# Half-rotary embedding on one core: all large transfers in one queue, six resident tiles, scratch in PSUM, tables loaded from GpSimd

## The chip, the cores and the metric

The kernel runs on one core of one Trainium2 chip. The metric is the device time of one execution in microseconds (us). The kernel before takes 162.42 us, the median of six runs (162.1 to 162.7).

A core has several engines that run side by side. Here only four matter: VectorE (DVE in the profile) does all the arithmetic; SyncE (its queue is SPq), ScalarE (ACTq) and GpSimd (POOL) issue transfers between the chip's main memory (DRAM) and the core's working memory (SBUF). Every transfer is cut into packets, which 16 DMA engines move. PSUM is a second, smaller memory of the core.

## The reference

`x` has 16 x 512 x 16 x 64 elements in float32 (33.55 MB); `cos` and `sin` have 512 x 32. Only the first 32 of the 64 elements of a head are rotated, and of each table only the first 16 columns are used. The other 32 elements are copied.

```python
batch, seq, heads, dim = x.shape          # 16, 512, 16, 64
half_dim = dim // 2                       # 32
x1, x2 = x[..., :half_dim], x[..., half_dim:]
cos = cos[None, :, None, :]; sin = sin[None, :, None, :]
rotated_first  = x1[..., :16] * cos[..., :16] - x1[..., 16:] * sin[..., :16]
rotated_second = x1[..., :16] * sin[..., :16] + x1[..., 16:] * cos[..., :16]
return np.concatenate([rotated_first, rotated_second, x2], axis=-1)
```

All of `x` must be read once and all of the output, which is as large, written once: 67.1 MB in all.

## The kernel before

**Tiling.** Each of the 128 partitions takes eight consecutive positions of the sequence (`K = 8`), that is 8 x 16 x 64 floats, 32 KB in one contiguous piece. A tile `x_t` is 128 such partitions, 4.19 MB (the profile's 4096 KB), and there are `T = 8` tiles. A tile goes in by one load (L58), is rotated in place, and goes out by one store (L73).

**Tables.** `cos` and `sin` are loaded into `stage`, 64 partitions x 1 KB each, by two transfers that ScalarE issues (L41, L42). Four copies on VectorE (L48) spread the 16 used columns over `table`, 128 partitions wide and with each set of columns twice in a row. `C` and `Sn` are views of it.

**Arithmetic.** Each tile is worked in two halves of `KC = 4` positions. For each half VectorE makes two products over 128 x 2048 elements, `a_t` = x1 x cos (L65) and `b_t` = x1 x sin (L66), and then a difference (L67) and a sum (L70) over 128 x 1024 elements, which write the rotated values back into `x_t`. `a_t` and `b_t` have one buffer each, in SBUF.

**Order and waits.** The program is written tile by tile, and every wait follows from the data. Loads are issued by SyncE, stores by ScalarE, so they lie in two queues: q1 holds the loads, q10 the stores and, ahead of them, the two table loads. Within one queue the order is that of issue. `x_t` has five buffers. So the first five loads need no buffer to come free, and load 5 (counting from 0) waits until store 0 has landed, load 6 for store 1, and load 7 for store 2.

**Names that the prediction uses.** Load t and store t are the transfers of tile t, L58 and L73 of the kernel before. "Landing" is the moment at which a transfer's completion is seen.

Of the kernel before, what the change touches and what calls it, by code (L numbers as in the profile page):

```python
# [1 line left out]

# [4 lines left out]


@with_exitstack
def kernel(  # L10
    ctx: ExitStack,
    tc: tile.TileContext,
    x: bass.AP,
    cos: bass.AP,
    sin: bass.AP,
    out: bass.AP,
):
    nc = tc.nc
    fp32 = mybir.dt.float32
    P = 128  # L20
    B, S, H, D = x.shape
    Q = D // 4
    HF = D // 2


    K = 8
    T = B * S // (P * K)
    PB = S // K
    REP = P // PB

    xf = x.rearrange("b s h d -> (b s h d)").rearrange("(t p f) -> t p f", t=T, p=P)
    of = out.rearrange("b s h d -> (b s h d)").rearrange("(t p f) -> t p f", t=T, p=P)
    cosf = cos.rearrange("(p k) j -> p (k j)", k=K)
    sinf = sin.rearrange("(p k) j -> p (k j)", k=K)

    const_pool = ctx.enter_context(tc.tile_pool(name="const", bufs=1))
    x_pool = ctx.enter_context(tc.tile_pool(name="xp", bufs=5))
    ab_pool = ctx.enter_context(tc.tile_pool(name="abp", bufs=1))

    stage = const_pool.tile([PB, 2, K, HF], fp32)  # L40
    nc.scalar.dma_start(out=stage[:, 0].rearrange("p k j -> p (k j)"), in_=cosf)  # L41
    nc.scalar.dma_start(out=stage[:, 1].rearrange("p k j -> p (k j)"), in_=sinf)  # L42


    table = const_pool.tile([P, 2, K, 2, Q], fp32)
    for r in range(REP):
        for t in range(2):
            nc.vector.tensor_copy(  # L48
                out=table[r * PB : (r + 1) * PB, t],
                in_=stage[:, t, :, 0:Q].unsqueeze(2).to_broadcast((PB, K, 2, Q)),  # L50
            )
    C = table[:, 0].rearrange("p k c j -> p k (c j)")
    Sn = table[:, 1].rearrange("p k c j -> p k (c j)")

    KC = 4
    for t in range(T):
        x_t = x_pool.tile([P, K, H, D], fp32)
        nc.sync.dma_start(out=x_t.rearrange("p k h d -> p (k h d)"), in_=xf[t])  # L58
        for k0 in range(0, K, KC):
            x1 = x_t[:, k0 : k0 + KC, :, 0:HF]  # L60
            c = C[:, k0 : k0 + KC].unsqueeze(2).to_broadcast((P, KC, H, HF))
            s = Sn[:, k0 : k0 + KC].unsqueeze(2).to_broadcast((P, KC, H, HF))
            a_t = ab_pool.tile([P, KC, H, HF], fp32)
            b_t = ab_pool.tile([P, KC, H, HF], fp32)
            nc.vector.tensor_mul(out=a_t[:], in0=x1, in1=c)  # L65
            nc.vector.tensor_mul(out=b_t[:], in0=x1, in1=s)  # L66
            nc.vector.tensor_sub(  # L67
                out=x1[:, :, :, 0:Q], in0=a_t[:, :, :, 0:Q], in1=b_t[:, :, :, Q:HF]
            )
            nc.vector.tensor_add(  # L70
                out=x1[:, :, :, Q:HF], in0=a_t[:, :, :, Q:HF], in1=b_t[:, :, :, 0:Q]
            )
        nc.scalar.dma_start(out=of[t], in_=x_t.rearrange("p k h d -> p (k h d)"))  # L73


# [1 line left out]
_INS = ['x', 'cos', 'sin']  # L77
_OUTS = [((16, 512, 16, 64), 'float32')]


# [23 lines left out]
```

## Time and profile before

| What | Value |
|---|---|
| Median of six runs | 162.42 us (162.1 to 162.7) |
| The profiled execution's own time | 162.44 us |
| Its span, from first to last instruction | 160.7 us, so that 1.7 us lie around it |
| VectorE busy | 110.8 us (69%), 68 instructions |
| One product over 128 x 2048 (L65, L66) | 2292 and 2285 ns |
| One difference or sum over 128 x 1024 (L67, L70) | 1226 and 1220 ns |
| Data moved | 33.69 MB read, 33.55 MB written, 419 GB/s over the span |
| Load of a tile, median from issue to landing | 33.9 us |
| Store of a tile, median from issue to landing | 31.3 us |
| Table loads, from issue to landing | 11.6 us (cos), 16.4 us (sin) |

The page of the profile cuts the span into 40 equal slices. In each slice a digit gives the busy share in tenths, for an engine or for the 16 DMA engines together, and the line GB/s gives what they moved. Bytes of a packet are counted where the packet starts, so that rates over very short stretches jump; over several microseconds they level out. The share of a queue is the time that its packets took, as a share of the time of 16 DMA engines.

### The profile page before, as it was taken

To read this page: it belongs to the slowest core of one execution; us is meant where nothing else is said; L and a number is where in the kernel's file an instruction comes from. 1 tells how busy PE (TensorE), PEld (TensorE's weight loads), DVE (VectorE), ACT (ScalarE), POOL (GpSimd) and SP (SyncE) were. 2 spreads that over 40 slices of the span, in tenths; PEclk is the share of its full clock that TensorE was granted. 3 is DMA by queue.
4 is the path that set the end of the run, shared out by engine and by line. 5 is a ranking of instruction groups with operands and counts; after the bars stand their busy time and mean duration, and the time that the engine had idled before them with its cause. 6 is when DMAs were issued, how large, how long until landed. Compare 5 with 4: busy or idle time off the path is not lost.

```text
span 160.7 us, 155 instructions
## 1 busy us (share of the span) xinstructions
DVE 110.8 (69%) x68; POOL 0.2 (0%) x4
## 2 busy tenths in 40 slices
DVE  0001599999999999999997799609994099940000
POOL 0000000000000000000000000000000000000000
DMA  7999999999999999999999999999999999999993
GB/s 237 424 400 408 392 465 441 400 465 441 400 449 457 400 416 473 416 392 498 416 392 481 432 392 465 449 392 465 434 400 465 441 400 457 449 400 449 441 416 139
DMA packets 2465, 67.25 MB, mean 419 GB/s; under 512 B 288, under 2 KB 416, under 8 KB 416
## 3 DMA queue, kind: packets, MB, share of 16 engines
q1 hardware_dynamic: 1152, 33.55, 49.2%
q10 hardware_dynamic: 1312, 33.69, 48.6%
q14 instruction: 1, 0.01, 0.0%
HBM read 33.69 MB, written 33.55 MB: 419 GB/s over the span
## 4 chain that ended last, share of the span: by engine, by line
DMA 53%; DVE 30%; issue 4%; DVEq 1%; ACTq 0%; SPq 0%
DMA x_t<-in_x_dram 21%; DMA out_dram<-x_t 21%; DVE b_t L66 11%; DMA stage<-in_sin_dram 10%; DVE a_t L65 10%; DVE x_t L70 5%; DVE x_t L67 4%; DVEq L99 1%; ACTq L41 0%; DVE table L48 0%; SPq L58 0%; DVEq L65 0%
## 5 line engine op out<-in xcount | busy, mean ns | idle before, releaser
L65 DVE TENSOR_TENSOR a_t<-x_t,table 128x2048 f32<-128x2048 f32 x16 | 36.7, 2292 | 13.8 <-DMA x_t<-in_x_dram 13.4
L66 DVE TENSOR_TENSOR b_t<-x_t,table 128x2048 f32<-128x2048 f32 x16 | 36.6, 2285 | 0.0
L67 DVE TENSOR_TENSOR x_t<-a_t,b_t 128x1024 f32<-128x1024 f32 x16 | 19.6, 1226 | 0.6
L70 DVE TENSOR_TENSOR x_t<-a_t,b_t 128x1024 f32<-128x1024 f32 x16 | 19.5, 1220 | 0.0
L48 DVE COPY table<-stage 64x256 f32<-64x256 f32 x4 | 1.1, 286 | 17.1 <-DMA stage<-in_cos_dram 12.4
L88 POOL MEMSET const-bfloat16-1.0<- 128x1 bf16 x1 | 0.1, 101 | 0.0
L88 POOL MEMSET const-uint8-127<- 128x1 uint8 x1 | 0.1, 101 | 0.0
L88 POOL MEMSET const-float32-0.0<- 128x1 f32 x1 | 0.1, 98 | 0.2 <-issue 0.2
L88 POOL MEMSET const-float32-1.0<- 128x1 f32 x1 | 0.1, 98 | 0.0
## 6 DMA issues: line engine op xcount, KB each, us to landing
x_t<-in_x_dram SPq DMA_DIRECT2D x8, 4096.0 KB, 33.9
out_dram<-x_t ACTq DMA_DIRECT2D x8, 4096.0 KB, 31.3
stage<-in_cos_dram ACTq DMA_DIRECT2D x1, 64.0 KB, 11.6
stage<-in_sin_dram ACTq DMA_DIRECT2D x1, 64.0 KB, 16.4
```

Of the source, the lines that this page charges most:

```text
L48: nc.vector.tensor_copy(out=table[r * PB : (r + 1) * PB, t], in_=stage[:, t, :, 0:Q].unsqueeze(2).to_broadcast((PB, K, 2, Q)),)
L65: nc.vector.tensor_mul(out=a_t[:], in0=x1, in1=c)
L66: nc.vector.tensor_mul(out=b_t[:], in0=x1, in1=s)
L67: nc.vector.tensor_sub(out=x1[:, :, :, 0:Q], in0=a_t[:, :, :, 0:Q], in1=b_t[:, :, :, Q:HF])
L70: nc.vector.tensor_add(out=x1[:, :, :, Q:HF], in0=a_t[:, :, :, Q:HF], in1=b_t[:, :, :, 0:Q])
L88: nc = _bacc.Bacc("TRN2", target_bir_lowering=False, num_devices=1)
L99: with _tile.TileContext(nc) as tc:
```

## The change

All tile transfers, loads and stores, are issued by SyncE into one queue. The first six loads are issued ahead of everything else. Then the order is store 0, store 1, load 6, store 2, load 7, store 3, and the remaining stores. Six buffers of `x_t` instead of five. Load 6 takes the buffer of tile 0 and so needs store 0, load 7 needs store 1.

`a_t` is gone: the product with sin comes first, into `b_t`, and the product with cos is then made in place in `x_t`. `b_t` lies in PSUM, with two buffers. The table loads are issued by GpSimd instead of ScalarE.

```diff
+    NB = 6
...
-    x_pool = ctx.enter_context(tc.tile_pool(name="xp", bufs=5))
-    ab_pool = ctx.enter_context(tc.tile_pool(name="abp", bufs=1))
+    x_pool = ctx.enter_context(tc.tile_pool(name="xp", bufs=NB))
+    b_pool = ctx.enter_context(tc.tile_pool(name="bp", bufs=2, space=bass.MemoryType.PSUM))
...
-    nc.scalar.dma_start(out=stage[:, 0].rearrange("p k j -> p (k j)"), in_=cosf)
-    nc.scalar.dma_start(out=stage[:, 1].rearrange("p k j -> p (k j)"), in_=sinf)
+    nc.gpsimd.dma_start(out=stage[:, 0].rearrange("p k j -> p (k j)"), in_=cosf)
+    nc.gpsimd.dma_start(out=stage[:, 1].rearrange("p k j -> p (k j)"), in_=sinf)
...
+    tiles = []
+
+    def load(t):
+        x_t = x_pool.tile([P, K, H, D], fp32, name="x_t")
+        nc.sync.dma_start(out=x_t.rearrange("p k h d -> p (k h d)"), in_=xf[t])
+        tiles.append(x_t)
+
+    for t in range(NB):
+        load(t)
     for t in range(T):
-        x_t = x_pool.tile([P, K, H, D], fp32)
-        nc.sync.dma_start(out=x_t.rearrange("p k h d -> p (k h d)"), in_=xf[t])
+        x_t = tiles[t]
         for k0 in range(0, K, KC):
...
-            a_t = ab_pool.tile([P, KC, H, HF], fp32)
-            b_t = ab_pool.tile([P, KC, H, HF], fp32)
-            nc.vector.tensor_mul(out=a_t[:], in0=x1, in1=c)
+            b_t = b_pool.tile([P, KC, H, HF], fp32)
             nc.vector.tensor_mul(out=b_t[:], in0=x1, in1=s)
+            nc.vector.tensor_mul(out=x1, in0=x1, in1=c)
             nc.vector.tensor_sub(
-                out=x1[:, :, :, 0:Q], in0=a_t[:, :, :, 0:Q], in1=b_t[:, :, :, Q:HF]
+                out=x1[:, :, :, 0:Q], in0=x1[:, :, :, 0:Q], in1=b_t[:, :, :, Q:HF]
             )
             nc.vector.tensor_add(
-                out=x1[:, :, :, Q:HF], in0=a_t[:, :, :, Q:HF], in1=b_t[:, :, :, 0:Q]
+                out=x1[:, :, :, Q:HF], in0=x1[:, :, :, Q:HF], in1=b_t[:, :, :, 0:Q]
             )
-        nc.scalar.dma_start(out=of[t], in_=x_t.rearrange("p k h d -> p (k h d)"))
+        nc.sync.dma_start(out=of[t], in_=x_t.rearrange("p k h d -> p (k h d)"))
+        if t >= 1 and t - 1 + NB < T:
+            load(t - 1 + NB)
```

## The prediction

> **What bounds the kernel now.** I read the busy shares in 40 slices first, then the queues, then windows of the transfers at the start, in the middle and at the end, and last the waits of VectorE.
>
> ```profile
> DVE  0001599999999999999997799609994099940000
> DMA  7999999999999999999999999999999999999993
> q1 hardware_dynamic: 1152, 33.55, 49.2%
> q10 hardware_dynamic: 1312, 33.69, 48.6%
> ```
>
> VectorE has holes and the DMA engines have none: only the first and the last slice are not full. The two queues' shares add up to 97.8% of 160.7 us, 157.2 us of packets. All that an order of transfers could win lies in the remaining 3.5 us and in packets that take longer than they must. The chain of waits names DMA (53%) and DVE (30%), but a share there doesn't make VectorE a bound: where the chain runs along VectorE (18 to 60 us), the DMA engines are full all the same.
>
> ```profile
> 0.00:1.60 1.60, 0.00 (x0) 0.20 (x4) 1.00 0.00 0
> 1.60:2.60 1.00, 0.00 (x0) 0.00 (x0) 1.00 1.92 524
> 2.60:3.50 0.90, 0.00 (x0) 0.00 (x0) 1.00 0.00 0
> ...
> 32.00:128.00 96.00, 82.38 (x49) 0.00 (x0) 1.00 1.00 432
> ...
> 158.50:160.70 2.20, 0.00 (x0) 0.00 (x0) 1.00 0.00 0
> ```
>
> In the windows the last two columns are DMA share and GB/s; a packet counts where it starts. Nothing starts for 1.6 us. Then 16 packets start (524 GB/s x 1 us = 16 x 32 KB), one for each engine, and the next only after 3.5 us. A packet usually takes 1.21 us (below), so the first takes about 0.7 us longer. In the middle 432 GB/s flow with loads and stores mixed: a tile of 4.19 MB, eight packets on each engine, takes 9.7 us. After 158.5 us nothing moves; those 2.2 us are the last store's completion and the program's end.
>
> What a packet costs, alone and mixed, is in the queues' view of four stretches (0 to 20, 20 to 35, 60 to 120, 142 to 158 us):
>
> ```profile
> q1 hardware_dynamic: 240, 7.34, 90.9%
> q10 hardware_dynamic: 160, 0.13, 2.0%
> ...
> q1 hardware_dynamic: 233, 6.59, 102.0%
> ...
> q10 hardware_dynamic: 448, 13.11, 50.6%
> q1 hardware_dynamic: 446, 13.04, 50.4%
> ...
> q10 hardware_dynamic: 224, 6.82, 98.6%
> ```
>
> Divide the bytes by 32,768 for the number of data packets; share x length x 16 engines is their time. Loads at the start: 0.909 x 20 x 16 / 224 = 1.299 us. Loads alone: 1.02 x 15 x 16 / 201 = 1.218. Mixed: stores 0.506 x 960 / 400 = 1.214, loads 0.504 x 960 / 398 = 1.216. Stores alone: 0.986 x 256 / 208 = 1.213. So a queue by itself runs at the speed of two, in either direction, within 0.4%.
>
> The sum for the kernel before: start 1.6, plus 128 packets on each engine x 1.214 = 155.4, plus the excess of the first 14 loads on each engine, 14 x 0.085 = 1.2, plus the tables' own packets, 2.0% of 20 us = 0.4, plus the end 2.2: 160.8, against the span of 160.7. Of the 1.2, about 0.7 is the first packet; the other 0.5 stands beside the tables' small packets.
>
> **What the Trainium skill says.** "DMA: Bandwidth & Descriptors", section "Issuing engines are not separate DMA queues": transfers from SyncE, ScalarE and GpSimd all run on the same 16 engines and interleave; several issuers save only issue time. The trace agrees (the prices above). Its section "Queues, rings and completion order": an engine goes round its queues packet by packet, and data descriptors carry no barrier. The trace agrees: 64 KB of cos land after 11.6 us, since each small packet waits for a packet of x. Its section "SWDGE vs HWDGE vs iDMA": GpSimd writes its descriptors in software, in packets of preferably up to 4096 bytes. No run here shows it yet. "VectorE: DVE Perf Modes", section "The perf-mode tier table": fp32 tensor_tensor with 2048 elements runs at one element per cycle, 2293 ns, from SBUF, and also at one with an operand in PSUM. The trace has 2292 ns for SBUF and nothing for PSUM.
>
> **The change part by part.** *One queue.* The bytes stay the same. I follow the order with 9.7 us a tile. Loads 0 to 5 fill the engines until 1.6 + 1.2 + 0.4 + 6 x 9.7 = 61 us. VectorE starts as before at 18.3 and needs 13.85 us a tile (2 x 6.93, from one L65 to the next but one half), so store 0 is issued at 32 and store 1 at 46, both before the loads run out: no hole. Store 0 moves from 61 to 71, store 1 to 81. Load 6 waits for store 0's landing: the last store lands at 142.4 + 17.4 = 159.8, some 1.5 us after its last packet, so load 6 is issued at about 73, 8 us ahead of store 1's end. What stands behind it on SyncE's queue is store 2, then load 7, and so on; none is due before 81. Store 2 was ready at 60 and is issued right after load 6. Load 6 moves until 90, store 2 until 100; load 7 waits for store 1's landing (82), is issued 18 us early, and moves until 110; stores 3, 4, 5, 6 end at 120, 129, 139, 149. Tile 4 is computed by 88, tile 5 by 101, tile 6 (load landed at 92) by 115, tile 7 (load landed at 112) by 129, against the 149 at which store 7 can begin. The engines have work throughout, with 20 us in hand at the end. Issue itself costs 0.34 us a transfer on SyncE and has those 8 us as cover. So the two long waits that go (loads for stores, 75.4 us in the queue's own waits; VectorE for loads, 13.4) were worth nothing: full DMA engines stood beside them, and what is late next is again the engines' work.
>
> Two small differences remain. Loads run alone for six tiles, 48 packets on each engine, instead of until 36 us, some 28: 20 x 0.004 = +0.1 us. And the direction turns inside one queue five times (load 5 to store 0, 1 to 6, 6 to 2, 2 to 7, 7 to 3). The trace has turns only between two queues, and there at every packet without cost. From below a turn costs nothing, since the mixed price is that of stores alone; from above, the pipeline empties as at the start, 0.7 us each, 3.5 in all. I take 0: descriptors have no barrier, and load follows load within 1.218 us a packet, completion included.
>
> *Tables from GpSimd.* Now they cost 0.4 of own packets and 0.5 of stretched neighbours. Fewer, larger packets would stretch fewer neighbours: from -0.9 (all inside the first packet's 0.7 us and the start) to +0.9 (software descriptors double it). I take -0.2, half of the stretching's share. If they land later, VectorE starts later: the cover is 20 us, so up to a start at 38 nothing happens. GpSimd's queue holds only its four memsets (0.2 us). What its set-up and close add outside the span I put at 0, at most 1 us.
>
> *Scratch in PSUM and the product in place.* Still four instructions a half with the same shapes. The difference waits for the product just before it, as now (gaps of 0.02 us). The sum may now wait for the difference and lose its 0.08 us of overlap: 16 x 0.08 = 1.3 us. Of the four, three touch PSUM; price 0, the upper end twice the duration (a gain would be hidden, so the lower end is 0 too). Under the 20 us of cover, three in each of 16 halves may each grow by 0.4 us before it counts. The sixth buffer costs nothing and only lets load 5 go early.
>
> Sum: +0.1 - 0.2 = -0.1 on the profiled 162.44, which stands at the median of 162.42: 162.3 us.
>
> **Rivals.** *A, the forecast: the transfers bound both, all packets at their old price.* 161.9 to 162.9 with the unknown of the tables and of GpSimd's close; chance 0.62, of it 0.17 faster, 0.30 the same, 0.15 slower. *B, slower: turns in one queue.* At each of the five turns a DMA engine drains before it reads the other way. At half the upper price, 0.35 us, +1.75: 164.1; at the full one 165.9. It decides from 0.09 us a turn. For it: the first packet's 0.7 us shows that filling the pipeline costs; against it: mixed packets have no excess. 0.20 with what a wait of SyncE may add in the same place. *C, faster: the tables hide in the start.* GpSimd issues at about the time of load 0, and its few packets pass under the first round: 162.4 - 0.9 = 161.5. For it: 0.9 us is what they cost now; against it: software descriptors come late. 0.13. *D, slower: PSUM makes VectorE the bound.* At twice the price, 16 x (2.29 + 1.23 + 1.22) = 76 us more, far past the cover: about 215. Against it: the skill's tier table. 0.02. *E, the order isn't as written,* say load 4 or 5 waits for the tables as load 4 does now (issued at 12.4, when cos had landed): before 40 us no hole, so no change; later, or with a dear close of GpSimd, about 163.2. 0.03.
>
> **How the numbers follow.** Two thousandths, 0.3 us, are about what can be told from no change here. Faster: 0.17 + 0.13 = 0.30. Same: 0.30. Slower: 0.15 + 0.20 + 0.02 + 0.03 = 0.40. The range takes in A, the inner half of C and most of B: 161.5 to 164.3; A's own is 161.9 to 162.9.
>
> **What would show it.** One queue with both directions at about 97% and slices full from second to last; packets at 1.213 to 1.218 us. A slice below 9 near 61, 81, 90, 100 or 110 us would show B; the transfers' start at 1.6 and the first 20 us show C; L65 to L70 above 2.7 or 1.6 us would show D. A hole while SyncE waits for a store would make my schedule wrong.

## The result, and the profile after

The changed kernel takes 162.91 us, the median of 35 runs (162.07 to 163.97), against 162.43 us for the kernel before (72 runs, 162.1 to 163.23). The ratio is 1.003, with a 95% interval of 1.0021 to 1.0039: slower by 0.3%, some 0.5 us. The profiled execution took 163.02 us, with a span of 161.2 us and so 1.8 us around it (1.7 before). Some runs of e7 (below) took up to 13 us more than its fastest, and the ratios leave such runs out.

The runs also spread more than those of the kernel before: the fastest are as fast as its fastest, and the slowest are 0.7 us slower than its slowest.

The page's slices and queues of the changed kernel, in the order of those shown for the kernel before:

```profile
DVE  0015999999999999999999999972999100000000
DMA  6999999999999999999999999999999999999993
...
q1 hardware_dynamic: 2304, 67.11, 97.5%
q0 software_dynamic: 64, 0.13, 0.2%
q14 instruction: 1, 0.01, 0.0%
```

VectorE has moved far ahead: it is finished at 125 us and not at 142. The DMA engines are as full as before, from the second slice to the last but one. One queue carries all 67.11 MB and takes 97.5% of the engines' time. With the tables' 0.2%, which lay in q10 before, that is 0.977 x 161.2 = 157.5 us of packets, against 157.2 before: the share is no larger, but the span is, and so the mean engine moves its packets for some 0.3 us longer. (Summed over the records of the packets, 157.57 against 157.11 us.) The tables are 64 packets in GpSimd's queue, q0: 32 with data of 4 KB each, where ScalarE's 128 held 1 KB each, and 32 that only signal completion.

Windows of the changed kernel (the last two columns are DMA share and GB/s), for the start, the middle and the end:

```profile
0.00:1.60 1.60, 0.00 (x0) 0.56 (x5) 1.00 0.00 0
1.60:2.60 1.00, 0.00 (x0) 0.80 (x2) 1.00 1.81 492
...
32.00:128.00 96.00, 89.43 (x55) 0.00 (x0) 1.00 1.00 431
158.50:161.20 2.70, 0.00 (x0) 0.00 (x0) 1.00 0.03 12
```

The start is the same, the middle moves 431 GB/s instead of 432, and a little still moves after 158.5 us. So the half microsecond is spread thin; no slice shows it. (A packet counts where it starts: before, none starts after 158.5 us, but the last one ends at 159.4.) SyncE's queue in the timeline shows that the order ran as the prediction laid it out:

```profile
72.65 0.34 SPq L61 DMA_DIRECT2D x_t<-in_x_dram  x1
73.08 0.51 SPq L81 DMA_DIRECT2D out_dram<-x_t  x1
82.43 0.34 SPq L61 DMA_DIRECT2D x_t<-in_x_dram  x1
```

Load 6 is issued at 72.65, store 2 right behind it, load 7 at 82.43. The prediction had 73 and 82.

**What the mean hides.** The page averages 16 DMA engines. The trace also holds every packet with its start, its duration and its queue. It doesn't name the engine, but packets that follow one another without a gap can be put into 16 chains, and nearly every chain has the 128 packets of `x` that one engine must move; each chain is taken for an engine. In every profile listed here the span ends 1.2 to 1.3 us after the last packet of the *slowest* engine (us from the start of the span):

```
kernel (profiled execution)      mean of the 16   slowest   span    packets over
                                 last packets     engine            1.25 us after 25 us
before                           158.51           159.41    160.65    1
changed                          159.08           160.02    161.25   22
changed, again                   158.88           160.00    161.19   14
e2  changed, two queues          158.76           159.46    160.75   17
e6  before, one queue            158.76           159.98    161.17   16
e11 changed, KC = 8              159.05           159.93    161.13   31
e12 before, KC = 8               160.13           161.22    162.40   99
e15 e12 with a pause             158.42           158.73    159.94    3
e17 changed, two queues, KC = 8  158.65           158.92    160.13   15
```

A packet of 32 KB normally takes 1.213 us. In the changed kernel 22 later ones take over 1.25 us. Eight of them are the last packet of load 6, directly ahead of store 2 (up to 1.555), two are the last packet of load 7, ahead of store 3 (up to 1.524). The others, around the turns from store to load above all, are 0.13 us longer at most, but for one behind a fetch of instructions (below). (A turn is a place in the one queue where it goes over from a load to a store or back.) In the second profile of the same kernel the longest of that kind is 1.599 us, again at the end of load 7. The slowest engine ends 0.6 us later than in the kernel before, and so does the span. The mean engine ends 0.57 us later too (0.37 in the second profile), so the loss isn't one of single engines alone.

Where the mean engine loses it can be read from the same records, as time of its load and store packets beyond 1.213 us each. From 36 us on, when the kernel before no longer moves loads alone, it is 0.05 us before and 0.33 us in the changed kernel (0.27 in its second profile). Of the 0.33 us, 0.19 lie in the packets next to a turn. Ahead of 25 us it is 1.20 and 1.42 us, but there single executions differ as much: e2 (below), with the same instructions up to there as the changed kernel, has 1.18 us, and the 16 profiles that are compared here reach from 1.03 to 1.57 us, whatever the kernel. So one profile tells nothing of a difference between kernels in that stretch.

### The profile page after: what moved, and what is told of

Read it like the earlier page. It is cut to its first block, busy times and chain, and to the rows that moved or that the text cites. A ratio compares the mean times of both kernels' runs of the same rounds, so it can differ in the third digit from the quotient of the medians.

```text
span 161.2 us, 150 instructions
## 1 busy us (share of the span) xinstructions
DVE 108.1 (67%) x68; POOL 1.4 (1%) x6
## 3 DMA queue, kind: packets, MB, share of 16 engines
q1 hardware_dynamic: 2304, 67.11, 97.5%
## 4 chain that ended last, share of the span: by engine, by line
DMA 52%; DVE 22%; issue 2%; DVEq 1%
DMA x_t<-in_x_dram 27%; DMA out_dram<-x_t 25%; DVE x_t L74 8%; DVE b_t L73 7%; DVE x_t L78 4%; DVE x_t L75 3%; DVEq L109 1%; DVEq L73 0%
## 5 line engine op out<-in xcount | busy, mean ns | idle before, releaser
L73 DVE TENSOR_TENSOR b_t<-x_t,table 128x2048 f32<-128x2048 f32 x16 | 36.1, 2305 | 5.9 <-DMA x_t<-in_x_dram 5.9
L74 DVE TENSOR_TENSOR x_t<-x_t,table 128x2048 f32<-128x2048 f32 x16 | 36.0, 2297 | 0.0
L75 DVE TENSOR_TENSOR x_t<-x_t,b_t 128x1024 f32<-128x1024 f32 x16 | 19.6, 1228 | 0.0
L78 DVE TENSOR_TENSOR x_t<-x_t,b_t 128x1024 f32<-128x1024 f32 x16 | 19.6, 1227 | 0.0
L42 POOL DMA_DIRECT2D stage<-in_cos_dram x1 | 0.6, 648 | 0.8 <-PEq L109 0.8
L43 POOL DMA_DIRECT2D stage<-in_sin_dram x1 | 0.5, 516 | 0.0
```

The source lines that it names most:

```text
L42: nc.gpsimd.dma_start(out=stage[:, 0].rearrange("p k j -> p (k j)"), in_=cosf)
L43: nc.gpsimd.dma_start(out=stage[:, 1].rearrange("p k j -> p (k j)"), in_=sinf)
L74: nc.vector.tensor_mul(out=x1, in0=x1, in1=c)
L75: nc.vector.tensor_sub(out=x1[:, :, :, 0:Q], in0=x1[:, :, :, 0:Q], in1=b_t[:, :, :, Q:HF])
L78: nc.vector.tensor_add(out=x1[:, :, :, Q:HF], in0=x1[:, :, :, Q:HF], in1=b_t[:, :, :, 0:Q])
```

## The experiments

Each row is the median of its own runs beside runs of the kernel before on the same chip; the ratio is to those.

| Run | What it is | us | Ratio to before, 95% interval |
|---|---|---|---|
| e1 | changed, tables from ScalarE | 162.90 | 1.0022 (1.0010 to 1.0034) |
| e2 | changed, stores from ScalarE: two queues | 162.53 | 1.0010 (1.0001 to 1.0019) |
| e4 | changed, eleven turns | 162.81 | 1.0031 (1.0013 to 1.0049) |
| e5 | changed, three turns | 163.42 | 1.0059 (1.0047 to 1.0071) |
| e3 | before, tables from GpSimd | 162.64 | 1.0014 (1.0006 to 1.0021) |
| e6 | before, one queue | 162.95 | 1.0032 (1.0020 to 1.0044) |
| e7 | before, tables in SyncE's queue | unclear | 1.0015 (0.9999 to 1.0032) |
| e10 | changed, again | 162.74 | 1.0029 (1.0015 to 1.0043) |
| e11 | changed, KC = 8 | 162.41 | 1.0000 (0.9987 to 1.0013) |
| e12 | before, KC = 8 | 164.18 | 1.0104 (1.0089 to 1.0118) |
| e13 | e12, one late engine | 164.47 | 1.0126 (1.0105 to 1.0147) |
| e14 | e11, one late engine | 162.65 | 1.0019 (1.0009 to 1.0029) |
| e15 | e12, pause of 0.8 us | 162.09 | 0.9980 (0.9972 to 0.9988) |
| e16 | e12, pause of 3.9 us | 162.29 | 0.9990 (0.9981 to 0.9999) |
| e17 | changed, two queues, KC = 8 | 162.22 | 0.9978 (0.9967 to 0.9989) |

### Which part of the change costs: e1, e2, e3, e6

e1 undoes the tables:

```diff
-    nc.gpsimd.dma_start(out=stage[:, 0].rearrange("p k j -> p (k j)"), in_=cosf)
-    nc.gpsimd.dma_start(out=stage[:, 1].rearrange("p k j -> p (k j)"), in_=sinf)
+    nc.scalar.dma_start(out=stage[:, 0].rearrange("p k j -> p (k j)"), in_=cosf)
+    nc.scalar.dma_start(out=stage[:, 1].rearrange("p k j -> p (k j)"), in_=sinf)
```

> The changed kernel with one part undone: ScalarE issues the two table loads again. Theory T (the tables from GpSimd stretch the load packets beside them by more than the tables from ScalarE did, and make the time spread): back to 162.4 to 162.6 us, and in the first 20 us the load packets cost 1.30 us as in the kernel before, not 1.32 to 1.33. Theory Q (the turns of direction inside one queue cost, and the tables do not): 162.8 to 163.0. Both in equal parts: about 162.7.

162.90 us: nothing that can be told from no change comes back (the intervals of 1.0022 and 1.0030 overlap widely). e2 undoes the one queue:

```diff
-        nc.sync.dma_start(out=of[t], in_=x_t.rearrange("p k h d -> p (k h d)"))
+        nc.scalar.dma_start(out=of[t], in_=x_t.rearrange("p k h d -> p (k h d)"))
```

> The changed kernel with another part undone: ScalarE issues the stores, so loads and stores lie in two queues; tables still from GpSimd. Theory Q: the packets of 60 to 120 us fall back to 1.213 us and the time to 162.5 or below. Theory T: stays at 162.8 to 163.0, with the same stretched packets in the first 20 us.

162.53 us, a ratio of 1.0010 instead of 1.0030: two thirds of the rise, 0.3 to 0.4 us, come back. The queues' view of 60 to 120 us shows what an average packet gains. First the changed kernel:

```profile
q1 hardware_dynamic: 884, 25.76, 99.8%
```

and then e2:

```profile
q1 hardware_dynamic: 444, 12.98, 50.1%
q10 hardware_dynamic: 444, 12.98, 50.1%
```

By the prediction's own division: one queue 0.998 x 960 / 786 = 1.219 us a packet, two queues 0.501 x 960 / 396 = 1.215. Over the 49 packets that each engine moves there, that is 0.2 us on the mean. How unevenly the engines lose it adds to this. e2's own packets over 1.25 us are another matter: one lies behind the fetch, the other 16 at the end of load 2, just ahead of store 0, which here starts while loads 3 to 5 are still to come. They may be what is left of the rise.

The same two parts, put alone into the kernel before. e3 changes only the tables' issuer there:

```diff
-    nc.scalar.dma_start(out=stage[:, 0].rearrange("p k j -> p (k j)"), in_=cosf)
+    nc.gpsimd.dma_start(out=stage[:, 0].rearrange("p k j -> p (k j)"), in_=cosf)
...
```

> The kernel before with one part of the change alone: GpSimd issues the two table loads. Theory U (single load packets are stretched, on some of the 16 DMA engines, where one queue goes over from a load to a store, and the slowest engine sets the end; the tables matter little): 162.4 to 162.6 us. Theory T (GpSimd's tables make the rise): 162.8 to 162.9.

162.64 against 162.40 us: a small rise, between the two theories' numbers. Its cause isn't shown. The tables land earlier, VectorE and store 0 begin earlier, and the last two packets of load 2, just ahead of store 0's first, are stretched by 0.27 us on the mean of the engines. But the profiled execution that shows this took 162.37 us, no longer than the kernel before. e6 makes only the one queue, with five loads ahead:

```diff
+    NB = 5
...
+    for t in range(NB):
+        load(t)
...
-        nc.scalar.dma_start(out=of[t], in_=x_t.rearrange("p k h d -> p (k h d)"))
+        nc.sync.dma_start(out=of[t], in_=x_t.rearrange("p k h d -> p (k h d)"))
+        if t >= 1 and t - 1 + NB < T:
+            load(t - 1 + NB)
```

> The kernel before with the other part alone: SyncE issues all tile transfers, five loads first, then two stores, then load and store in turn; five buffers, scratch in SBUF, tables from ScalarE as before. Theory U: 162.8 to 163.0 us, the runs spread over more than 1 us, and the stretched packets are last packets of loads that a store follows. Theory V (the sixth buffer, the earlier VectorE or PSUM has a part in it): 162.4 to 162.6.

162.95 us, the whole rise by itself, without the sixth buffer, PSUM or GpSimd. The spread that was expected did not show in its five runs (162.71 to 163.07). In its profile the slowest engine loses 0.45 us at the last packet of load 7, ahead of store 4; it is also the engine with the fetch of instructions (below).

A third pair of kernels that differ in the one queue alone is e11 and e17 (below, both with `KC = 8`): 1.0000 with one queue, 0.9978 with two. And the profiles agree beyond single medians. From 36 us on, the packets of the mean engine take 0.26 to 0.41 us too long in all eight one-queue profiles (changed, e10, e1, e4, e5, e6, e11, e14), and 0.01 to 0.06 us in six of the eight two-queue profiles (before, e2, e3, e15, e16, e17). The other two are e12 and e13, of which more below.

### Is it the number of turns? e4 and e5

e4 has three loads ahead and then turns at every transfer, e5 puts loads 6 and 7 together:

```diff
# e4
-    for t in range(NB):
+    for t in range(3):
...
-        if t >= 1 and t - 1 + NB < T:
-            load(t - 1 + NB)
+        if t + 3 < T:
+            load(t + 3)
# e5
-        if t >= 1 and t - 1 + NB < T:
-            load(t - 1 + NB)
+        if t == 1:
+            load(NB)
+            load(NB + 1)
```

> The changed kernel with three loads ahead instead of six, then store and load in turn from the first store on: eleven turns of direction in the one queue instead of five, and a shorter stretch of loads alone. Theory Q (about 0.05 us a turn on every DMA engine, more on single ones): 6 more turns, +0.2 to +0.5 us, 163.1 to 163.4. Theory T: no more than the changed kernel's 162.9; the stretch of loads alone shrinks by 24 packets of 4 ns, -0.1.

> The changed kernel with loads 6 and 7 one after the other behind store 1: three turns of direction instead of five. Theory Q: -0.1 to -0.2 us, 162.7 to 162.8. Theory T: 162.9. If SyncE's wait for store 1 ahead of load 7 opened a hole at 91 us, a slice there would fall below 9 and the time would rise by as much.

Eleven turns: 162.81 us, no more than five. Three turns: 163.42 us, clearly more in the median of its five runs, and no hole (SyncE issued load 7 at 82.41). A fixed price for each turn is refuted. Neither theory's number was met by both: e5 cost 0.5 us more than either had it. In e5's profile 11 of the 16 engines stretch the last packet of load 7, by 0.16 us on the mean and 0.63 on the worst; in e4 the last packets of loads 2 and 6 are the worst, while loads 3, 4, 5 and 7 lose 0.03 us or less there on the mean. A turn may cost an engine nothing or half a microsecond.

### Chance or fixed? e10

The changed kernel once more, without an edit.

> The changed kernel once more, for a second profile and on the chip of these runs. Theory U: 162.9 us again, with stretched packets once more in last packets of loads ahead of a store, but on other DMA engines than in the first profile; the span ends 1.2 us after the last packet of the slowest engine. If the same engines are late by the same amount, it is a fixed feature of the order, not chance.

162.74 us on this chip, ratio 1.0029. The number of stretched packets at the end of load 6 is now one, not eight, and six engines stretch its first packet; at the end of load 7 it is three. Both profiles have a slowest engine that ends at 160.0, by different sums. All these places are turns. Which turn is hit, on how many engines and by how much changes from one execution to the next; since the records don't name the engines, whether the same ones are hit can't be told.

### One late engine, and the fetch of instructions: e11 to e14

The line q14 of the page is one packet of 8 KB in the middle of the span: the records show it at 112.5 us before and at 97.0 us after. It takes 0.31 us on one engine, and the packet of `x` that follows on that engine takes 1.799 us (before) and 1.666 us (after). That engine sets the end of the kernel before, and in the second profile of the changed kernel too, where it loses another 0.39 us at the end of load 7. I took this for a rule, that a late engine loses more in one queue. e11 and e12 take the fetch away, by half as many instructions on VectorE:

```diff
-    KC = 4
+    KC = 8
```

(e11 also gives `b_t` one buffer instead of two; each is now twice as large.)

> The changed kernel with each tile worked in one pass (KC = 8, half as many VectorE instructions, one buffer of 16 KB in PSUM). Theory W (one DMA engine has to fetch 8 KB of instructions at about 97 us, which costs it 0.3 us and stretches its next packet by 0.4 to 0.6; it is then behind the others, and one queue makes an engine that is behind lose more at each turn from load to store, since it alone is still on its load): with no fetch in the span the time falls to 162.2 to 162.5 us. Theory X (the turns cost whatever is late): no change, 162.8 to 162.9.

> The kernel before with the same KC = 8: two queues and no fetch of instructions in the middle. Theory W: the slowest engine loses its 0.9 us and the next slowest sets the end some 0.5 us earlier: 161.8 to 162.0 us, which would beat both kernels. Theory X: 162.4.

e11's queues have no line for instructions any more:

```profile
q1 hardware_dynamic: 2304, 67.11, 97.5%
q0 software_dynamic: 64, 0.13, 0.2%
```

and its time is 162.41 us, that of the kernel before. e12 missed by 2 us: 164.18. Two queues and no fetch, and slower than any kernel so far. Its queues' view of 60 to 120 us shows the loss in the loads alone:

```profile
q1 hardware_dynamic: 442, 12.91, 51.6%
q10 hardware_dynamic: 434, 12.65, 48.9%
```

A load packet takes 0.516 x 960 / 394 = 1.257 us there, a store packet 0.489 x 960 / 386 = 1.216. e13 and e14 add to e12 and e11 one transfer for one engine alone:

```diff
+    late = const_pool.tile([1, 2039], fp32)
...
+        if t == 1:
+            nc.vector.tensor_copy(out=late[:, 0:1], in_=x_t[0:1, 0, 0, 0:1])
+            nc.scalar.dma_start(out=late, in_=xf[0][0:1, 0:2039])
```

> The two-queue kernel of KC = 8 with one more transfer, which the result doesn't use: 8 KB into one partition after tile 1, so that it lies on one DMA engine alone and makes it late by 0.7 to 0.9 us. Theory W: a late engine stays as late as it is, +0.4 to +0.8 us against the same kernel without it. Theory X: the same.

> The one-queue kernel of KC = 8 with the same added transfer on one DMA engine, after tile 1 and so ahead of all turns. Theory W: the late engine loses another 0.3 to 0.5 us at two or three turns from load to store, so +1.0 to +2.0 us against the same kernel without it, and the packets that are stretched at the turns are those of this engine. Theory X: no more than with two queues, +0.4 to +0.8.

+0.29 us with two queues, which the intervals can't tell from nothing, and +0.24 with one, both less than any theory had it. The added packet also did less than it was meant to: it took 0.31 us, and the packet behind it 0.14 us (e13) and 0.01 us (e14) more than usual, so that the engine in e14 was late by 0.3 us and not by 0.7 to 0.9. That engine lost 0.09 us at most at a later turn and ended at 158.84 us, close to the mean engine's 158.85, while another, which was not made late, set the end at 159.67. So the rule found no support.

For an engine as late as the fetch makes it, the rule wasn't tested: in e5, e6 and e10 it is the engine with the fetch that has the longest stretch at the end of load 7. Other pairs speak against the rule. Without the fetch the one-queue kernel goes from 1.0030 to 1.0000 (e11), the one with two queues from 1.0010 to 0.9978 (e17): the gain is the same. And e11, which meets theory W's number, still stretches last packets of loads by up to 0.45 us, with no fetch to make an engine late.

### What decides the stretch: e15, e16, e17

The records of single engines show how e12 differs from the kernel before. L4.1 is packet 1 of load 4, S1.0 packet 0 of store 1; in brackets, what a packet took beyond 1.213 us, in ns:

```
before, one engine:  L3.7 S0.5 S0.6 L4.0 S0.7 L4.1 L4.2 S1.0 L4.3 S1.1
e12,    one engine:  L3.7 S0.6 S0.7 L4.0 L4.1(+458) S1.0 L4.2 S1.1 L4.3(+108) S1.2
e15,    one engine:  L3.7 S0.5 S0.6 L4.0 S0.7 L4.1 L4.2 S1.0 L4.3 S1.1
```

In e12 the stores lie one packet earlier against the loads: store 0 is issued at 31.50 us instead of 32.15, and its first packet comes after two packets of load 3, not three. From there on each new store begins one packet closer to the beginning of a load than in the kernel before, on 10 to 13 of the 16 engines, and packets 1 and 2 of loads 4 to 7 are stretched (0.29 to 0.46 us a load, on the mean of the engines). To test whether that phase (where among the packets of a load the stores begin) is the cause, e15 and e16 only pause VectorE ahead of the first product:

```diff
+    pause = const_pool.tile([P, 2, K, 2, Q], fp32)
+    for r in range(2):          # 8 in e16
+        nc.vector.tensor_copy(out=pause[:], in_=table[:])
     KC = 8
```

> The kernel before with KC = 8 and two copies on VectorE between the tables and the first product, which nothing uses: 0.7 us of pause, so that store 0 is issued at 32.2 us, as in the kernel before, and not at 31.5. Theory P (a load packet is stretched where a store's first packet falls next to the load's own beginning; the phase between the two queues decides): the stretched packets are gone and the time is 161.8 to 162.2 us. Theory K (long VectorE instructions stretch the packets): 164.2 as without the pause.

> The same with eight such copies, some 3 us of pause: store 0 is issued at about 34.5 us and begins in the middle of load 3. Theory P: no stretched packets, 161.8 to 162.2 us (the pause itself is hidden, since VectorE has to wait for loads 5 to 7 in any case). Theory K: 164.2.

> The changed kernel with two queues (stores issued by ScalarE) and KC = 8: six buffers, PSUM, tables from GpSimd, no fetch of instructions in the span. Theory P: store 0 begins at about 31 us, beside the end of load 2, where the same kernel with KC = 4 had no stretch after the first store: 162.0 to 162.2 us. Theory K: 163.5 or more.

e15: a pause of 0.8 us makes the kernel 2 us *faster* (1.0104 to 0.9980), 162.09 us. The timeline of ScalarE's queue in e12, store 0 and then store 1:

```profile
31.50 0.35 ACTq L73 DMA_DIRECT2D out_dram<-x_t  x1
44.83 0.34 ACTq L73 DMA_DIRECT2D out_dram<-x_t  x1
```

and in e15:

```profile
32.27 0.35 ACTq L76 DMA_DIRECT2D out_dram<-x_t  x1
45.60 0.34 ACTq L76 DMA_DIRECT2D out_dram<-x_t  x1
```

and its queues at 60 to 120 us:

```profile
q10 hardware_dynamic: 448, 13.11, 50.6%
q1 hardware_dynamic: 448, 13.11, 50.6%
```

Loads and stores are back at 0.506 x 960 / 400 = 1.214 us. e16 (store 0 at 35.41) has six packets over 1.25 us in all after 25 us, e17 none once store 0 has begun (its 15 lie at the end of load 2); the times of both, 162.29 and 162.22, lie a little above what was expected. So theory K is refuted: the instructions are as long as in e12, and the stretch is gone. Of theory P this much is shown: with two queues, a shift of VectorE's work and of the stores by 0.8 us makes or removes the stretch. (The pause moves both, so the runs don't tell VectorE's part from the stores'.) That the place of a store's first packet among the load's packets decides it, engine by engine, is not shown, and the records speak against it. In e12 store 1 begins on three engines after packet 2 of load 4, as in the kernel before, and just these lose 0.64 to 0.71 us there. In e2, e3 and e17 stores 1 to 5 begin at the same places of a load as store 0, and only store 0 has a stretched packet ahead of it.

e15 and e17 are also faster than the kernel before, by 0.2%: without the fetch, and without the stretch that e12 has.

### One that decided nothing: e7

```diff
-    nc.scalar.dma_start(out=stage[:, 0].rearrange("p k j -> p (k j)"), in_=cosf)
...
+    nc.sync.dma_start(out=x_0.rearrange("p k h d -> p (k h d)"), in_=xf[0])
+    nc.sync.dma_start(out=stage[:, 0].rearrange("p k j -> p (k j)"), in_=cosf)
...
```

> The kernel before with its two queues, but SyncE issues the table loads between load 0 and load 1, so that their small packets come one after the other and not each between two packets of x. If the stretched neighbours in the first 20 us are the interleaving's price (0.5 us on every engine), 161.9 to 162.1 us; if the small transfers cost the same wherever they lie, 162.4.

Its 23 runs reach from 162.27 to 175.7 us, and the interval of its ratio from no change to 0.3% slower. The gain that was expected did not come, and where the tables are best placed stays open.

## Why the prediction was wrong, step by step

The forecast was 162.3 us, 0.1 us less than before, with all packets at their old price; measured are some 0.5 us more. That 162.91 us lies in the range given, 161.5 to 164.3, is due to the width of the range and not to its sum.

*What bounds it.* Right. Full DMA engines before and after; VectorE's end 17 us earlier, and all waits of loads for stores and of VectorE for loads that went, were worth nothing.

*The order and its cover.* Right, to within 0.6 us for both loads whose issue was named, and store 7 still starts at 149 us. No hole. VectorE did not start as before at 18.3 us, but at 14.5: from GpSimd the tables land 7.7 and 10.0 us after their issue, not 11.6 and 16.4. That lay off the path.

*Loads alone.* Right: 20 to 35 us has, in the changed kernel, this line,

```profile
q1 hardware_dynamic: 225, 6.32, 98.0%
```

which is 0.98 x 240 / 193 = 1.219 us a packet, as before (1.218). The sum left out that in one queue loads 6 and 7 run alone as well, 16 more packets on each engine; at its 0.004 us each that is less than 0.1 us.

*PSUM and the product in place.* Right in its cost of nothing:

```profile
L73 DVE TENSOR_TENSOR b_t<-x_t,table 128x2048 f32<-128x2048 f32 x16 | 36.1, 2305 | 5.9 <-DMA x_t<-in_x_dram 5.9
L74 DVE TENSOR_TENSOR x_t<-x_t,table 128x2048 f32<-128x2048 f32 x16 | 36.0, 2297 | 0.0
L75 DVE TENSOR_TENSOR x_t<-x_t,b_t 128x1024 f32<-128x1024 f32 x16 | 19.6, 1228 | 0.0
L78 DVE TENSOR_TENSOR x_t<-x_t,b_t 128x1024 f32<-128x1024 f32 x16 | 19.6, 1227 | 0.0
```

The product that writes PSUM takes 2305 ns (2285 into SBUF), the difference and the sum that read it 1228 and 1227. The Trainium skill, "VectorE: DVE Perf Modes", section "The perf-mode tier table", agrees: fp32 tensor_tensor runs at the same tier, one element a cycle, with operands in SBUF (2293 ns there for 2048 elements) and with one in PSUM. The instructions did not come in the order that the prediction took, though: with two buffers of `b_t` the two halves of a tile are interleaved, so that no product is used by the instruction right behind it, and a tile takes 13.33 us instead of 13.85. Rival D is out.

*Tables.* Taken at -0.2 us. With them undone the changed kernel keeps its time within the intervals (e1): no gain shows. In the first 20 us their packets take 1.8% instead of 2.0%. The load packets there, in the changed kernel and then in e2, with the same tables from GpSimd:

```profile
q1 hardware_dynamic: 240, 7.34, 92.0%
...
q1 hardware_dynamic: 240, 7.34, 90.8%
```

That is 0.920 x 320 / 224 = 1.314 and 0.908 x 320 / 224 = 1.297 us a packet, on both sides of the 1.299 before: fewer neighbours are stretched, each by more, and the sum isn't smaller. Rival C is out. Alone in the kernel before the tables cost 0.24 us (e3), perhaps by way of an earlier store 0, which the prediction counted as free.

*Turns in one queue.* This is the step that failed: "I take 0: descriptors have no barrier, and load follows load within 1.218 us a packet, completion included." Load follows load, and store follows store, but a load that a store follows may stretch its last packet. So may, by less, the packets on either side of a turn back to a load. The runs show, in place of the 0, that one queue costs 0.3 to 0.4 us (e2 against the changed kernel, e17 against e11) to 0.55 us (e6 against the kernel before). Rival B's "against it: mixed packets have no excess" held for two queues and was carried over to one, of which no trace was at hand. Rival B named the place; its price for each turn, 0.35 us, and the sum over turns are not what the runs show (e4, e5).

*The form of the sum.* It added packets at the price of a mean engine, and closed on the span of the kernel before, 160.8 against 160.7, by a misreading: "after 158.5 us nothing moves" is true of starts only. The mean engine ends at 158.51 us, the slowest, the one with the fetch, at 159.41, and 1.24 us follow; the 2.2 us that were taken for completion and the program's end contain 0.9 us by which that engine is late. A stretch of 0.1 us on the mean at the end of load 6 (changed kernel) is 0.34 us on the engine that ends last, and such sums on single engines set the end. Both show in the result: the mean engine ends later, and the slowest is as far behind it as before or farther (0.9 us before, 0.9 and 1.1 us in the changed kernel's two profiles).

What stays open: what inside the DMA engines makes a load's packet longer just ahead of a store's first packet, and why a turn in one queue sometimes has it and sometimes not. Whether the tables have a share in the rise, about 0.1% by e2 and e3, stays open too. The phase could be shifted for two queues only; in one queue it can't be moved, since the store always begins right where the load ends.

## What to carry to other kernels

With the DMA engines full, an order that removed waits won nothing here, and what remained was decided below the page's averages: look at single packets and at the slowest of the engines, and multiply a share by its span before you call it the same. Two queues, one for each direction, were the better form here, but only with the stores in a good phase: an edit that sped up an engine off the path cost 1% (e12), where it started the stores 0.65 us earlier, and a pause of 0.8 us won it back (e15). Before a slower result is put down to the edit itself, shift the phase and run again.

## What the runs showed that I had not expected

- A fetch of 8 KB of instructions, one packet in the page's line q14, makes one DMA engine 0.7 to 1.0 us late (0.31 for itself, 0.35 to 0.66 on the next packet), and in a kernel bound by transfers that engine can set the end: it did in the profiles of the kernel before, e1, e2, e3, e5, e6 and e10, and not in the first profile of the changed kernel or in e4. Half as many VectorE instructions made it go away; the changed kernel went from a ratio of 1.003 to 1.000 with it, and with two queues from 1.001 (e2) to 0.998 (e17).
- Interleaving the two halves on VectorE saves 0.5 us a tile (13.33 against 13.85 us) without any instruction being shorter. It won nothing here.
